# Weight sums of two pairs in single slots, sums of x begun earlier, key tiles copied by one engine

## The chip, the cores and the metric

The program runs on one NeuronCore of a Trainium2 chip, with float32 inputs and outputs. Five engines run side by side: TensorE (PE in the views; PEld is its weight load), VectorE (DVE), ScalarE (ACT), GpSimd (POOL) and SyncE (SP, which here only issues transfers). The metric is the device time of one execution in microseconds; a kernel is told by the median of its runs.

## What is computed

Two layers of one mixer, on x of 512 rows by 1024. `jnp.split(z, ...)` cuts one wide projection into three token mixers, three gate paths and the merge logits.

```python
for l in range(DEPTH):                                   # 2
    z = jnp.einsum('bsd,de->bse', x, w_in[l])
    (q_lat, kv_lat, k_pe, g_mla, lru_u, g_lru,
     r_q, r_k, r_v, g_ret, merge_logits) = jnp.split(z, IN_SPLITS, axis=-1)
    y_mla = _mla(...) * jax.nn.silu(g_mla)               # attention, 8 heads, keys from a latent
    y_lru = _rglru(...) * jax.nn.silu(g_lru)
    y_ret = _retention(r_q, r_k, r_v, ...) * jax.nn.silu(g_ret)
    gates = jax.nn.sigmoid(merge_logits + b_merge[l]).reshape(B, S, N_BRANCHES, D_MODEL)
    mixed = (gates[:, :, 0] * jnp.einsum('bse,ed->bsd', y_mla, w_branch[l, 0])
             + gates[:, :, 1] * jnp.einsum('bse,ed->bsd', y_lru, w_branch[l, 1])
             + gates[:, :, 2] * jnp.einsum('bse,ed->bsd', y_ret, w_branch[l, 2]))
    out = jnp.einsum('bsd,de->bse', mixed, w_out[l])
    x = _layer_norm(DEEPNORM_ALPHA * x + out, ln_g[l], ln_b[l])
```

## The kernel before

**Products.** A float32 product is made of three matmuls of a shorter float type (`mm3`, L138 to L140): each operand is split into a high part, a cast by ScalarE (L113), and the rest, a subtraction by VectorE (L114). Weights arrive in raw tiles (`wr`, `ws`) and leave as `wh` and `wl`.

**Stages of a layer.** Latent projections, the recurrence, the attention (query tiles, then four key tiles `psk`, L641 to L645, whose two heads each are copied to `kt` by VectorE, L644, and by ScalarE, L645), the retention, and then 14 pairs of tiles for the merge gates and one gate path, each gate pair with its branch projection `psb`, and the output projection.

**The retention** is the loop of six passes at L791. Pass q makes tile q of keys and queries (`ret_in`: two projections into `psmm`, each turned by `rope`, four VectorE operations whose temporaries `rsw` and `rt` are slots), then for tile q-1 the transposes, scores `sd` and states (`ret_keys`, `ret_states`), then for tile q-2 the output (`ret_out`, into `por`, copied to `yr` by ScalarE at L789). The values `vr` lie in a wide tile and are read by the last `por`. In passes 4 and 5 the loop also makes the sums of x, two steps each.

**The pairs.** `in_pair` (L445) makes two tiles of 512 columns as seven block products in place of eight, in the way of Strassen and Winograd: into `psx`, `psy1` and `psz`, from blocks of x and of the weights and from sums of such blocks. The sums of x are common to all pairs: `x_sums` (L329) builds them in a scratch tile `sx` by VectorE additions (L341, L344; four chunks of 256 columns at once) and splits them into `tx` and, the last, into a free part of `xth`, `xtl`. The first gate pair needs them one after another. Between products ScalarE or VectorE fetches `psx`; the copy L468 is one such fetch, and the next product into `psx` waits for it.

**The sums of weights** are made per pair by `Blocks` (L370). `load` issues on SyncE the two raw halves `ws` (L395, L396), then on GpSimd an accumulating transfer that adds a third block to them (L398 for both halves at once, 512 KB; L401 one half each, 256 KB), and on SyncE the raw tiles `wr` (L405, L409 for the branch weights `wbr`, L412). `make` splits one block after another in the order a11, a12, s1, s2, b1, s3, b0, a22, s4; the cast of s1 is the first to read the accumulated `ws`. Casts run up to six blocks (`AHEAD`) in front of the products. Pair 0 has its raw sums in two slots. Pairs 1, 2, 3, ... share one wide tile, `self.two`, half of it each.

**What sets the order.** Tiles come from pools: 13 slots of 128 x 512, five wide tiles (four slots each), four half ones, three `wr`, four pairs `wh`/`wl`, three PSUM buffers for `psmm`, `por`, `psx` and the like. A tile waits until the last reader of its buffer's former content is done. The order on each engine is the order of the program with priorities: weight loads and their splits are pulled forward (L840 for the first pair). Every engine works strictly in its order, so an instruction that waits holds up all behind it.

Of the kernel before, what the change touches and what calls it, by code (L numbers as in the profile page):

```python
# [12 lines left out]
F32R = mybir.dt.float32r  # L13
# [10 lines left out]
KD = D // P  # L24
# [43 lines left out]
HS = S // 2  # L68
# [5 lines left out]
def trunk(ctx, tc, x_in, xt_in, pos, vecs, wg, wt, wrv, wuq, wuk, wuv, wlru, wbr, wout, lng, lnb, dec, rett, out):  # L74
    nc = tc.nc
# [18 lines left out]
    def slot(name, dt=F32):  # L94
        return tmp.tile([P, S], dt, tag="slot", name=name, bufs=NSLOT)

    def wide(name, dt=F32):
        return tmp.tile([P, NST, S], dt, tag="wide", name=name, bufs=NWIDE)

    def half(name, dt=F32):  # L100
        return tmp.tile([P, 4, S], dt, tag="half", name=name, bufs=4)

    def PS(n):
        if n in SS:
            return ps_s.tile([P, S], F32, tag="s", name=n)
        return ps_mm.tile([P, S], F32, tag="mm", name=n)

    def raw(t):
        return t.bitcast(F32)


    def split(hi, lo, src):
        nc.scalar.copy(hi, src)  # L113
        nc.vector.tensor_tensor(out=lo, in0=src, in1=raw(hi), op=ALU.subtract)  # L114
# [51 lines left out]
    def v(l, col, n=1):  # L166
        return vec[:, l * NV + col:l * NV + col + n]
# [139 lines left out]
    def layer(l):  # L307
# [13 lines left out]
        tx = [None] * 4  # L321
# [4 lines left out]
        def sums(i):  # L326
            return [(tx[i][0][:, j, :], tx[i][1][:, j, :]) for j in range(HK)]

        def x_sums(t1, t2, t3, scratch):  # L329


            tx[:3] = [(t[:, :, :HS], t[:, :, HS:]) for t in (t1, t2, t3)]
            tx[3] = (xth[:, :HK, HS:], xtl[:, :HK, HS:])
            r1, r2 = scratch[:, :, :HS], scratch[:, :, HS:]

            def b(k, t):
                o = (slice(None), slice(HK * k, HK * k + HK), slice(HS * t, HS * t + HS))
                return raw(xth[o]), raw(xtl[o])

            def sub(out, a, c, op=ALU.subtract):  # L340
                nc.vector.tensor_tensor(out=out, in0=a, in1=c, op=op)  # L341

            def neg_less(out, a, c):
                nc.vector.scalar_tensor_tensor(out=out, in0=a, scalar=-1.0, in1=c[0], op0=ALU.mult, op1=ALU.subtract)  # L344
                sub(out, out, c[1])

            def less(out, a, c):
                sub(out, a[0], c[0])
                sub(out, out, a[1], ALU.add)
                sub(out, out, c[1])  # L350

            def one():
                less(r1, b(0, 0), b(0, 1))
                split(tx[0][0], tx[0][1], r1)

            def two():
                neg_less(r2, r1, b(1, 1))
                split(tx[1][0], tx[1][1], r2)

            def three():  # L360
                less(r1, b(1, 1), b(0, 1))
                split(tx[2][0], tx[2][1], r1)

            def four():
                neg_less(r2, r2, b(1, 0))
                split(tx[3][0], tx[3][1], r2)

            return [one, two, three, four]

        class Blocks:  # L370
# [10 lines left out]
            def load(self):  # L381
                n = self.loaded
                if n == len(self.pairs):
                    return
                self.loaded += 1
                t, wb = self.pairs[n]
                d = {}
                if n == 0:
                    s0, s1 = slot("ws0"), slot("ws0")
                elif n == 1:  # L390
                    self.two = wide("ws")
                if n:
                    s = self.two[:, n % 2 * 2:n % 2 * 2 + 2, :]
                    s0, s1 = s[:, 0, :], s[:, 1, :]
                nc.sync.dma_start(out=s0, in_=wt[l, t + 1][:, 512:])  # L395
                nc.sync.dma_start(out=s1, in_=wt[l, t][:, :512])  # L396
                if n:
                    nc.gpsimd.dma_start(out=s, in_=wt[l, t + 1][:, :512].unsqueeze(1).to_broadcast([P, 2, 512]), accum_op=ALU.add)  # L398
                else:
                    for sn in (s0, s1):  # L400
                        nc.gpsimd.dma_start(out=sn, in_=wt[l, t + 1][:, :512], accum_op=ALU.add)  # L401
                d["s1"] = d["s2"] = d["s4"] = s0
                d["s3"] = s1
                r = wraw.tile([P, 1024], F32, tag="wr", name="wr")
                nc.sync.dma_start(out=r, in_=wt[l, t])  # L405
                d["a11"], d["a12"] = r[:, :512], r[:, 512:]
                if wb is not None:
                    r = wraw.tile([P, 1024], F32, tag="wr", name="wr")
                    nc.sync.dma_start(out=r, in_=wb)  # L409
                    d["b0"], d["b1"] = r[:, :512], r[:, 512:]  # L410
                d["a22"] = slot("wr2")
                nc.sync.dma_start(out=d["a22"], in_=wt[l, t + 1][:, 512:])  # L412
                self.raws.append(d)
# [110 lines left out]
        for g in range(2 if l else 0):  # L524
            chunks = lat_weights(l, g)
            if g == 0:
                for st in range(NST):
                    ps = PS("psg0")
# [25 lines left out]
        for c in range(4):  # L554
            ps = in_tile(T_U + c)
            cw = V_CW + 4 * c
            nc.vector.tensor_scalar(out=xc[:, c, :], in0=ps, scalar1=v(l, cw + 3), scalar2=v(l, V_CB + c), op0=ALU.mult, op1=ALU.add)
            for j in range(3):
                d = 3 - j
# [3 lines left out]
        for b in range(5):  # L563
            ps = ps_t.tile([P, S], F32, tag="t", name="psl")
# [11 lines left out]
        ps = ps_t.tile([P, S], F32, tag="t", name="pskp")  # L576
# [5 lines left out]
        for b in range(8):  # L582
            c = b // 2
            q, o = (slice(0, 64), slice(64, 128)) if b % 2 == 0 else (slice(64, 128), slice(0, 64))
# [3 lines left out]
            ps = PS("psr")  # L588
# [29 lines left out]
        kt = [kth[h // 4][:, h % 4, :] for h in range(H)]  # L618
# [3 lines left out]
        for c in range(3):  # L622
            hi, lo = load_w(wuq[l, c], 768)
            for j in range(2):
                t = 2 * c + j
                ps = PS("psq2" if t % 2 else "psq")
# [12 lines left out]
        for t in range(4):  # L639
            ps = PS("psk")  # L640
            for k in range(2):  # L641
                w = slice((t * 2 + k) * P, (t * 2 + k + 1) * P)
                mm3(ps, (hi[:, w], lo[:, w]), kvlat[k], k == 0, k == 1)
            nc.vector.tensor_copy(kt[2 * t][0:64, :], ps[0:64])  # L644
            nc.scalar.copy(kt[2 * t + 1][0:64, :], ps[64:128])  # L645
        hi, lo = load_w(wuv[l], 1024)
        for st in range(NST):
            sl = slice(st * P, (st + 1) * P)
            ps = PS("psvm")
# [71 lines left out]
        steps = [(h, i) for h in range(H) for i in range(NST)]  # L721
# [22 lines left out]
        def ret_in(t):  # L744
            rts[t] = half("rt")
            rope(rts[t][:, 1, :], in_tile(T_RK + t), cos_r, sin_r)
            rope(rts[t][:, 0, :], in_tile(T_RQ + t), cos_r, sin_r)
# [43 lines left out]
        for q in range(6):  # L791
            if q < 4:
                ret_in(q)
            if 0 <= q - 1 < 4:
                ret_keys(q - 1)
                ret_states(q - 1)
            if 0 <= q - 2 < 4:
                ret_out(q - 2)
            if q >= 4:
                if q == 4:  # L800
                    steps = x_sums(wide("tx", F32R), wide("tx", F32R), half("tx", F32R), half("sx"))
                steps[2 * q - 8]()
                steps[2 * q - 7]()


        mixed = [slot("mixed") for _ in range(KD)]
        mixhl = {}

        def branch_mm(w, j, ys):
# [34 lines left out]
        def gate_pair(b, d2, ys, mh=None):  # L844
            gts = [slot("gt") for _ in range(2)]
            bias = [v(l, V_BM + b * KD + 2 * d2 + j) for j in range(2)]
            psb = {}

            def gate(i, part, src):
                if i == 0:  # L850
                    nc.scalar.activation(gts[0], gts[0], AF.Sigmoid, bias=bias[0])
                    return
                nc.scalar.activation(gts[1][:, part], src, AF.Sigmoid, bias=bias[1], scale=-1.0)
                nc.scalar.activation(gts[1][:, HS:], gts[1][:, HS:], AF.Sigmoid, bias=bias[1], scale=-1.0)

            def branch(j):
                psb[j] = branch_mm(bs.take(), 0, ys)

            in_pair(bs, gts, gate, branch)
            for j in (1, 0):  # L860
                d, gt = 2 * d2 + j, gts[j]
                if b == 1:
                    nc.vector.tensor_tensor(out=mixed[d], in0=psb[j], in1=gt, op=ALU.mult)
                    continue
                nc.vector.tensor_tensor(out=gt, in0=psb[j], in1=gt, op=ALU.mult)
                nc.vector.tensor_tensor(out=mixed[d], in0=mixed[d], in1=gt, op=ALU.add)
                if b == 2:
                    ml = slot("ml", F32R)
                    split(mh[:, d % 4, :], ml, mixed[d])
                    mixhl[d] = (mh[:, d % 4, :], ml)  # L870
# [41 lines left out]
        for d2 in range(4):  # L912
            if d2 % 2 == 0:
                mh = half("mh", F32R)
            if d2 in (1, 2):
                t = tmp.tile([P, 2, 1024], F32, tag="wide", name="wor", bufs=NWIDE)
# [8 lines left out]
        for n, c in enumerate(WO):  # L925
            if c in WO_W:
                dst = None
            elif c in WO_X:
                t = tmp.tile([P, 2, 1024], F32R, tag="wide", name="wow", bufs=NWIDE)
# [18 lines left out]
        for st in range(NST):  # L948
# [11 lines left out]
            for g, (c0, c1) in enumerate(cuts):  # L960
                n = c1 - c0
                if pss:
                    ps = pss[g]
                    out_mm(ps, sl, c0, n, (KD - 1, KD - 2), (False, True))
                else:
                    ps = ps_mm.tile([P, S], F32, tag="mm", name="pso")[:, :n]
# [18 lines left out]
    for l in range(DEPTH):  # L985
        layer(l)
# [85 lines left out]
```

## Time and profile before

| | |
|---|---|
| median of 3 runs | 1059.83 us (1059.24 to 1062.46) |
| the profiled execution | 1059.59 us |
| its span, first to last instruction | 1057.8 us |
| busy: PE, PEld, DVE, ACT, POOL | 97%, 86%, 78%, 51%, 10% |
| chain that ended last: PE, DVE, ACT, issue, DMA | 76%, 10%, 8%, 3%, 3% |
| mean granted TensorE clock | 0.993 |

Busy time is an average over stages that differ. A stage is read from its waits: a wait of PE names the engine and the line that ended it, the timeline gives its place, and the chain of waits tells what that one waited for in turn. The granted clock is 1.00 at 2.4 GHz and 0.50 at 1.2 GHz; a window's value is the mean.

### The profile page before, as it was taken

To read this page: it belongs to the slowest core of one execution; us is meant where nothing else is said; L and a number is where in the kernel's file an instruction comes from. 1 tells how busy PE (TensorE), PEld (TensorE's weight loads), DVE (VectorE), ACT (ScalarE), POOL (GpSimd) and SP (SyncE) were. 2 spreads that over 40 slices of the span, in tenths; PEclk is the share of its full clock that TensorE was granted. 3 is DMA by queue.
4 is the path that set the end of the run, shared out by engine and by line. 5 is a ranking of instruction groups with operands and counts; after the bars stand their busy time and mean duration, and the time that the engine had idled before them with its cause. 6 is when DMAs were issued, how large, how long until landed. Compare 5 with 4: busy or idle time off the path is not lost.

```text
span 1057.8 us, 16761 instructions
## 1 busy us (share of the span) xinstructions
PE 1029.3 (97%) x6279; PEld 907.2 (86%) x6279; DVE 821.3 (78%) x1608; ACT 539.5 (51%) x1025; POOL 109.0 (10%) x161
## 2 busy tenths in 40 slices
PE   9999999999699999999999999999998999999997
PEld 8878788889599999998898787888887999999986
DVE  6988988667796787787646888985688877877765
ACT  4659577621555465463124695775225555555610
POOL 1200012100002200100002000121000022001000
PEclk9999999999899999999999999999999999999999
DMA  8612523552476556545136225136516754666311
GB/s 256 170 70 85 160 81 81 123 118 59 120 210 169 150 159 189 144 136 172 63 131 158 80 81 168 56 81 149 117 34 166 207 149 141 165 210 170 125 64 60
DMA packets 52081, 138.26 MB, mean 131 GB/s; under 512 B 5664, under 2 KB 8608, under 8 KB 52000
## 3 DMA queue, kind: packets, MB, share of 16 engines
q1 hardware_dynamic: 39744, 106.44, 30.3%
q0 software_dynamic: 11968, 30.41, 16.4%
q8 instruction: 49, 0.80, 0.3%
q10 hardware_dynamic: 288, 0.34, 0.2%
q14 instruction: 32, 0.26, 0.1%
HBM read 130.88 MB, written 4.19 MB: 128 GB/s over the span
## 4 chain that ended last, share of the span: by engine, by line
PE 76%; DVE 10%; ACT 8%; issue 3%; DMA 3%; SPq 0%; DVEq 0%; ACTq 0%; POOLq 0%
PE psx L138 5%; PE psx L139 5%; PE psx L140 5%; PE psmm L138 5%; PE psmm L140 5%; PE psmm L139 5%; PE psb L138 4%; PE psb L139 4%; PE psb L140 4%; PE pso L139 3%; PE pso L140 3%; PE pso L138 3%; PE psz L138 3%; PE psz L140 2%; PE psz L139 2%
## 5 line engine op out<-in xcount | busy, mean ns | idle before, releaser
L113 ACT CAST wh<-wr 128x512 fp32r<-128x512 f32 (+5 forms) x188 | 133.5, 723 | 124.4 <-PE psmm L139 42.2
L114 DVE TENSOR_TENSOR wl<-wr,wh 128x512 fp32r<-128x512 f32 (+5 forms) x188 | 151.8, 818 | 30.3 <-ACT wh L113 29.6
L138 PE MATMUL psmm<-xth,wh 128*128 128x512 f32 x320 | 125.9, 393 | 0.0
L139 PE MATMUL psmm<-xtl,wh 128*128 128x512 f32 x320 | 125.1, 391 | 0.0
L140 PE MATMUL psmm<-xth,wl 128*128 128x512 f32 x320 | 124.7, 390 | 0.0
L113 ACT CAST wh<-ws 128x512 fp32r<-128x512 f32 x112 | 69.4, 620 | 89.6 <-PE psx L139 38.5
L114 DVE TENSOR_TENSOR wl<-ws,wh 128x512 fp32r<-128x512 f32 x112 | 77.1, 689 | 43.9 <-ACT wh L113 43.0
L138 PE MATMUL psx<-xth,wh 128*128 128x256 f32 x224 | 65.3, 292 | 10.2 <-ACT gt L468 10.1
L140 PEld LDWEIGHTS psmm<-xth,wl 128*128 128x128 f32 x320 | 60.1, 188 | 12.5
L138 PEld LDWEIGHTS psmm<-xth,wh 128*128 128x128 f32 x320 | 60.1, 188 | 12.2
L139 PEld LDWEIGHTS psmm<-xtl,wh 128*128 128x128 f32 x320 | 60.1, 188 | 11.8
L138 PE MATMUL psx<-tx,wh 128*128 128x256 f32 x224 | 64.2, 286 | 2.5 <-ACT tx L113 2.3
L139 PE MATMUL psx<-xtl,wh 128*128 128x256 f32 x224 | 64.6, 288 | 0.0
L140 PE MATMUL psx<-xth,wl 128*128 128x256 f32 x224 | 63.9, 287 | 0.0
L140 PE MATMUL psx<-tx,wl 128*128 128x256 f32 x224 | 63.4, 283 | 0.0
L139 PE MATMUL psx<-tx,wh 128*128 128x256 f32 x224 | 63.3, 283 | 0.0
L398 POOL DMA_DIRECT2D ws<-in_wt x26 | 31.2, 1200 | 305.9 <-DMA ws<-in_wt 233.5
L138 PEld LDWEIGHTS psx<-xth,wh 128*128 128x128 f32 x224 | 43.7, 195 | 12.9 <-ACT gt L468 11.1
L138 PEld LDWEIGHTS psx<-tx,wh 128*128 128x128 f32 x224 | 42.8, 191 | 6.1 <-ACT tx L113 3.2
L139 PEld LDWEIGHTS psx<-xtl,wh 128*128 128x128 f32 x224 | 44.1, 197 | 1.0
L139 PEld LDWEIGHTS psx<-tx,wh 128*128 128x128 f32 x224 | 42.8, 191 | 1.3
L140 PEld LDWEIGHTS psx<-xth,wl 128*128 128x128 f32 x224 | 43.6, 195 | 0.2
(310 smaller groups left out, 3079.3 us busy)
## 6 DMA issues: line engine op xcount, KB each, us to landing
wr<-in_wt SPq DMA_DIRECT2D x68, 512.0 KB, 3.7
ws<-in_wt SPq DMA_DIRECT2D x56, 256.0 KB, 3.0
ws<-in_wt POOLq DMA_DIRECT2D x26, 512.0 KB, 6.7
wr<-in_wbr SPq DMA_DIRECT2D x24, 512.0 KB, 4.6
wl<-in_wt POOLq DMA_DIRECT2D x22, 512.0 KB, 6.3
wr<-in_wt SPq DMA_DIRECT2D x28, 256.0 KB, 3.6
wr<-in_wrv SPq DMA_DIRECT2D x8, 512.0 KB, 3.3
wor<-in_wout SPq DMA_DIRECT2D x8, 512.0 KB, 5.8
```

The costliest lines, as they stand in the source:

```text
L113: nc.scalar.copy(hi, src)
L114: nc.vector.tensor_tensor(out=lo, in0=src, in1=raw(hi), op=ALU.subtract)
L138: nc.tensor.matmul(ps, lh, rh, start=start, stop=False, skip_group_check=more)
L139: nc.tensor.matmul(ps, lh, rl, start=False, stop=False, skip_group_check=more)
L140: nc.tensor.matmul(ps, ll, rh, start=False, stop=stop, skip_group_check=more)
L398: nc.gpsimd.dma_start(out=s, in_=wt[l, t + 1][:, :512].unsqueeze(1).to_broadcast([P, 2, 512]), accum_op=ALU.add)
```

## The change

Three things. The raw weight sums of pair 1, like those of pair 0, are put in two slots with an accumulating transfer each; the wide tile begins with pair 2. `x_sums` takes its tiles one after another where they are first written and is spread over passes 2 to 5 of the retention, one step each, with the steps cut a little differently. The VectorE copy of the key tiles becomes a ScalarE copy. Also, the slots of `mixed` are taken when they are written.

```diff
-        def x_sums(t1, t2, t3, scratch):
-            tx[:3] = [(t[:, :, :HS], t[:, :, HS:]) for t in (t1, t2, t3)]
+        def x_sums(scratch):
             tx[3] = (xth[:, :HK, HS:], xtl[:, :HK, HS:])
...
+            def parts(i, t, r):
+                tx[i] = (t[:, :, :HS], t[:, :, HS:])
+                split(tx[i][0], tx[i][1], r)
             def one():
                 less(r1, b(0, 0), b(0, 1))
-                split(tx[0][0], tx[0][1], r1)
+                parts(0, wide("tx", F32R), r1)
+                neg_less(r2, r1, b(1, 1))
             def two():
-                neg_less(r2, r1, b(1, 1))
-                split(tx[1][0], tx[1][1], r2)
+                less(r1, b(1, 1), b(0, 1))
             def three():
-                less(r1, b(1, 1), b(0, 1))
-                split(tx[2][0], tx[2][1], r1)
+                parts(2, half("tx", F32R), r1)
+                parts(1, wide("tx", F32R), r2)
...
-                if n == 0:
+                if n < 2:
                     s0, s1 = slot("ws0"), slot("ws0")
-                elif n == 1:
+                elif n == 2:
                     self.two = wide("ws")
-                if n:
+                if n >= 2:
                     s = self.two[:, n % 2 * 2:n % 2 * 2 + 2, :]
...
-                if n:
+                if n >= 2:
                     nc.gpsimd.dma_start(out=s, in_=wt[l, t + 1][:, :512].unsqueeze(1).to_broadcast([P, 2, 512]), accum_op=ALU.add)
                 else:
                     for sn in (s0, s1):
...
-            nc.vector.tensor_copy(kt[2 * t][0:64, :], ps[0:64])
+            nc.scalar.copy(kt[2 * t][0:64, :], ps[0:64])
             nc.scalar.copy(kt[2 * t + 1][0:64, :], ps[64:128])
...
-            if q >= 4:
-                if q == 4:
-                    steps = x_sums(wide("tx", F32R), wide("tx", F32R), half("tx", F32R), half("sx"))
-                steps[2 * q - 8]()
-                steps[2 * q - 7]()
-        mixed = [slot("mixed") for _ in range(KD)]
+            if q == 2:
+                steps = x_sums(half("sx"))
+            if q >= 2:
+                steps[q - 2]()
+        mixed = {}
...
                 if b == 1:
+                    mixed[d] = slot("mixed")
                     nc.vector.tensor_tensor(out=mixed[d], in0=psb[j], in1=gt, op=ALU.mult)
```

The changed kernel's lines stand some three to five lower from there on (L398 and L399 load `ws`, L404 accumulates one half, L471 is the copy that was L468).

SyncE's queue in the last passes of layer 1's retention, before (`ws_2808` and `ws_2809` are pair 0's slots, `ws` the wide tile; `wr_2818` and `wr_2903` are the second raw tiles of pairs 0 and 1):

```order
L395 DMA ws_2808<-in_wt 128x512
L396 DMA ws_2809<-in_wt 128x512
L412 DMA wr_2818<-in_wt 128x512
L412 DMA wr_2903<-in_wt 128x512
L395 DMA ws<-in_wt 128x512
L396 DMA ws<-in_wt 128x512
L395 DMA ws<-in_wt 128x512
L396 DMA ws<-in_wt 128x512
L409 DMA wr<-in_wbr 128x1024
```

and now (`ws_2800`, `ws_2801` for pair 0, `ws_2887`, `ws_2888` for pair 1):

```order
L398 DMA ws_2800<-in_wt 128x512
L399 DMA ws_2801<-in_wt 128x512
L415 DMA wr_2810<-in_wt 128x512
L398 DMA ws_2887<-in_wt 128x512
L399 DMA ws_2888<-in_wt 128x512
L415 DMA wr_2897<-in_wt 128x512
L398 DMA ws<-in_wt 128x512
L399 DMA ws<-in_wt 128x512
L398 DMA ws<-in_wt 128x512
L399 DMA ws<-in_wt 128x512
L412 DMA wr<-in_wbr 128x1024
```

Pair 1's two loads stand ahead of the wide tile's, which are now those of pairs 2 and 3; the loads into `ws_2887` and `ws_2888` wait for reads of rope temporaries on VectorE. Pair 1's branch weights stay behind all of them.

VectorE in the retention, from the scores `sd` of one tile to the next rope, before (`state_120`: that tile's states):

```order
L764 TENSOR_TENSOR sd<-psrs,tabs 128x512 x2
L775 COPY state_120<-pskv 64x64
L755 TENSOR_TENSOR rt<-rt,tabs 128x384
L777 SCALAR_TENSOR_TENSOR state_120<-state_120,retd,pskv 64x64 x2
L775 COPY state_120<-pskv 64x64
L777 SCALAR_TENSOR_TENSOR state_120<-state_120,retd,pskv 64x64 x2
L234 STREAM_SHUFFLE rsw<-psmm 128x512
```

and now, from the same `sd` to the same rope:

```order
L767 TENSOR_TENSOR sd<-psrs,tabs 128x512 x2
L778 COPY state_120<-pskv 64x64
L340 TENSOR_TENSOR sx<-sx,xtl 128x4x256
L780 SCALAR_TENSOR_TENSOR state_120<-state_120,retd,pskv 64x64
L343 SCALAR_TENSOR_TENSOR sx<-sx,xth 128x4x256
L780 SCALAR_TENSOR_TENSOR state_120<-state_120,retd,pskv 64x64
L778 COPY state_120<-pskv 64x64
L114 TENSOR_TENSOR tx<-sx,tx 128x4x256
L780 SCALAR_TENSOR_TENSOR state_120<-state_120,retd,pskv 64x64
L340 TENSOR_TENSOR sx<-sx,xtl 128x4x256
L780 SCALAR_TENSOR_TENSOR state_120<-state_120,retd,pskv 64x64
L234 STREAM_SHUFFLE rsw<-psmm 128x512
```

Three sums and a split have come in between the states of one tile and the rope of the next (the rope that starts at 244.51 us in the trace of before).

ScalarE around the copy L468 (now L471) of pair 0, before:

```order
L113 CAST wh<-ws 128x512
L113 CAST xth<-sx 128x4x256
L468 COPY gt<-psx 128x256
L113 CAST wh<-wr 128x512
L853 ACT_TABLE_LOAD
```

and now:

```order
L113 CAST xth<-sx 128x4x256
L113 CAST wh<-wr 128x512
L113 CAST wh<-ws_2800 128x512
L113 CAST wh<-wr_2810 128x512
L113 CAST wh<-wr 128x512
L113 CAST wh<-ws_2800 128x512
L467 COPY gt<-psx 128x256
L113 CAST wh<-wr 128x512
L113 CAST wh<-ws_2887 128x512
L471 COPY gt<-psx 128x256
L113 CAST wh<-wr 128x512
```

The cast of the last sum of x (`xth<-sx`) has moved ahead of most of pair 0's casts; the cast of pair 1's s1 still stands in front of the copy, and reads a slot now.

## Rows read from the trace of the kernel before

**Rows 1.** The page's first part: busy us, share of the span, instructions.

```profile
PE 1029.3 (97%) x6279; PEld 907.2 (86%) x6279; DVE 821.3 (78%) x1608; ACT 539.5 (51%) x1025; POOL 109.0 (10%) x161
```

**Rows 2.** Waits of PE: waiter, what ended the wait, us in total, times, longest.

```profile
PE psx L138 <- ACT gt L468: 10.1, 2, 6.4
PE psx L138 <- ACT tx L113: 2.3, 2, 1.2
PE psb L140 <- DVE wl L114: 2.1, 2, 1.0
PE psk L138 <- ACT kt L645: 1.4, 2, 0.7
```

**Rows 3.** Timeline of PE: start, us, what, [idle before it and its releaser].

```profile
277.64 0.40 PE L138 MATMUL psb<-yl,wh 128*128 128x512 f32 x1
277.88 0.39 PE L139 MATMUL psb<-yl,wh 128*128 128x512 f32 x1
...
285.02 0.58 PE L138 MATMUL psx<-xth,wh 128*128 128x256 f32 x1 [6.40 <-ACT gt L468]
...
808.00 0.58 PE L138 MATMUL psx<-xth,wh 128*128 128x256 f32 x1 [3.67 <-ACT gt L468]
```

**Rows 4.** The chain that ended last, 250 to 300 us: start, us, what.

```profile
269.47 4.61 DMA ws<-in_wt
...
274.61 8.50 DMA ws<-in_wt
...
283.65 1.04 ACT xth L113
```

**Rows 5.** Timeline of ScalarE, 283 to 301 us.

```profile
283.13 0.62 ACT L113 CAST wh<-ws 128x512 fp32r<-128x512 f32 x1 [6.61 <-DMA ws<-in_wt]
...
284.60 0.36 ACT L468 COPY gt<-psx 128x256 f32<-128x256 f32 x1
...
299.74 0.38 ACT L468 COPY gt<-psx 128x256 f32<-128x256 f32 x1 [1.05 <-PE psx L140]
```

**Rows 6.** Windows: us, busy us per engine (instructions), granted clock, DMA share, GB/s.

```profile
250.00:255.00 5.00, 5.00 (x48) 4.72 (x46) 5.00 (x10) 1.04 (x1) 0.00 (x0) 1.00 0.01 3
...
285.00:290.00 5.00, 4.98 (x25) 4.77 (x26) 4.89 (x8) 2.75 (x5) 0.00 (x0) 0.63 0.01 1
805.00:810.00 5.00, 2.00 (x7) 1.78 (x8) 2.29 (x3) 3.64 (x5) 0.00 (x0) 0.75 0.85 193
810.00:815.00 5.00, 5.00 (x40) 5.00 (x40) 4.40 (x9) 2.88 (x6) 0.00 (x0) 0.91 0.00 0
```

**Rows 7.** Timeline of VectorE in the retention and the first gate pair.

```profile
233.73 0.01 DVE L234 LOAD_MASK_SELECT rsw<-psmm  x1 [1.47 <-PE psmm L140]
...
244.51 0.01 DVE L234 LOAD_MASK_SELECT rsw<-psmm  x1 [4.64 <-PE psmm L140]
...
248.49 2.48 DVE L341 TENSOR_TENSOR sx<-sx,xtl 128x1024 f32<-128x1024 f32 x2
...
267.75 0.29 DVE L777 SCALAR_TENSOR_TENSOR state<-state,retd,pskv 64x64 f32<-64x64 f32 x1
...
274.47 1.23 DVE L114 TENSOR_TENSOR tx<-sx,tx 128x1024 fp32r<-128x1024 f32 x1
```

**Rows 8.** Waits of SyncE's queue, 200 to 300 us, columns as in rows 2.

```profile
SPq L395 <- PE por L788: 21.4, 1, 21.4
```

**Rows 9.** Timeline of GpSimd, 225 to 300 us.

```profile
274.61 1.21 POOL L398 DMA_DIRECT2D ws<-in_wt  x1 [31.99 <-DMA ws<-in_wt]
```

**Rows 10.** Transfers by issue, 225 to 300 us: count, KB each, median us to landing.

```profile
ws<-in_wt POOLq DMA_DIRECT2D x2, 256.0 KB, 5.0
```

**Rows 11.** Timeline of PE at the keys; instructions on `kt`: ns lowest/median/highest.

```profile
128.54 0.50 PE L138 MATMUL psk<-lh,wh 128*128 128x512 f32 x1 [0.72 <-ACT kt L645]
...
L644 DVE COPY kt<-psk x8: 671/682/685, 127.2 to 656.0; 64x512 f32<-64x512 f32 x8
L645 ACT COPY kt<-psk x8: 575/582/583, 127.9 to 657.2; 64x512 f32<-64x512 f32 x8
```

## Prediction

> **What bounds the kernel now.** I read the page's busy line first: PE is busy 1029.3 of 1057.8 us [rows 1], so the kernel can gain where TensorE stands still or runs at its lower clock, and hardly anywhere else. Next come the waits of PE, grouped by what ended them [rows 2]. Four groups are worth more than 1.3 us, each has two members (one per layer), and together they hold 10.1 + 2.3 + 2.1 + 1.4 = 15.9 us. Three of them stand in the first two gate pairs after the retention, the fourth in the key projection of the attention. The reader should then find the largest in the timeline: a 6.40 us hole before 285.02 in layer 1 and a 3.67 us hole before 808.00 in layer 2 [rows 3]. The matmul behind each hole takes 0.58 us, and the windows say why: the granted clock is 0.63 as a mean over 285 to 290 us, and 0.75 and 0.91 over 805 to 815 [rows 6], where the stretches ahead have 1.00. So a hole costs its length and some time at the lower level (1.2 GHz) behind it.
>
> What fills the hole is in the chain [rows 4]: SyncE's load of the raw halves of pair 1 starts only at 269.47 and takes 4.61 us, GpSimd's accumulating transfer starts at 274.61 and takes 8.50 us. ScalarE's cast of that sum starts at 283.13 after 6.61 us of nothing, and behind it on the same engine stand the cast of the last sum of x (1.04 us) and the copy L468 that TensorE needs [rows 4, 5]. Why the issue is so late is in SyncE's waits: 21.4 us for the last `por` of the retention [rows 8], since the wide tile takes over the buffer of `vr`, which is read until then.
>
> **1. Pair 1 in slots.** It removes one 512 KB accumulating transfer per layer and adds two of 256 KB; SyncE's two loads stay. The loads no longer wait for `vr`: a slot comes free when a rope temporary has been read. By the order of the changed kernel these are two ropes of the last passes: before, the first ends at 247.3 us (one 1.22 us sum ahead of the two from 248.49, [rows 7]), the second, one rope on, at 253.4. Chain: 253.4 + 4.61 + 0.5 (the gap between landing and issue in [rows 4]) + 5.0 [rows 10] = 263.5 us, with 8.5 [rows 4] in place of 5.0 at worst 267. The cast stands just ahead of the copy (before: L468, 284.6), and TensorE is ready for what follows at 278.6, so the sum is wanted by about 276. Cover: 9 to 12 us. The holes go: 6.40 + 3.67 = **10.1 us**.
>
> The lower clock goes with them. In 285 to 290 PE worked 4.98 us at 0.63: 0.37 x 4.98 = 1.8 us. In layer 2 the 2.00 us busy before 810 ran at half speed (0.58 us matmuls, [rows 3]), 1.0 us, and 0.09 x 5 = 0.45 up to 815: together 1.5. **3.3 us** [rows 6].
>
> A rule that speaks against this part: the Trainium skill (DMA: Bandwidth & Descriptors, SWDGE vs HWDGE vs iDMA) says that GpSimd writes the descriptor rings into SBUF, and GPSIMD Engine Reference (the table of its specifications) says that it shares its SBUF interface with VectorE and contends with VectorE's instructions of two SBUF inputs. Pair 1's issues move from 274.6 to about 251 and 258, where such instructions fill VectorE. The row: VectorE is busy 5.00 of 5 us in 250 to 255 [rows 6], but the issue at 274.61 took 1.21 us while such an instruction ran beside it, from 274.47 for 1.23 us [rows 7, 9]. By the rule the issue could end only behind a run of these, some 5 us later, and the cover still holds; by the row it is free. The sum is the same, the chance of rival A is not.
>
> **2. Sums of x, one step per pass from the third.** Nothing is removed: twelve VectorE operations of 1.22 us per layer and four splits move. What they stand in for: VectorE waits 4.64 us before 244.51 and 1.47 us before 233.73 for `psmm` [rows 7]. The new order puts two sums (2.4 us) before the second of these ropes and three sums and a split (3 x 1.22 + 1.23 = 4.9 us) into the first-named gap, so the rope at 244.51 comes (2.4 - 1.5) + (4.9 - 4.6) = 1.2 us late, and catches up behind it, where three sums (3.7 us) stood and two stand now. Three `mm` buffers lie between rope and TensorE; whether 1.2 us gets through I can't read, so I bound it by 0 and 1.2 per layer.
>
> At the other end, before the last state, the old order has two tx-sized operations, the sums and four operations of pair 0's weights; it ends the state at 268.0 (267.75 + 0.29, [rows 7]). Adding up the new rows from 255.0 by the same durations I get 265, so `por`, and with it the buffer of `vr`, comes about 3 us sooner. The last two products of pair 0 then find their operands made: the wait on the cast of tx (2.3 us, both layers) and that on `wl` of pair 0 (2.1 us), which was queued behind the sums on VectorE, go: **4.4 us** [rows 2]. New short waits at `por` and `psz`, where a sum now stands between states: I bound them by 0 and two sums per layer (2.4 us) and take 0.45, near the lower end, since TensorE had no wait at all on these states before [rows 2].
>
> **3. Keys by ScalarE alone.** VectorE loses four copies of 0.68 us per layer, ScalarE gains four of 0.58 [rows 11]. A tile of keys is two copies, 1.16 us in a row, against the 6 matmuls of TensorE; matmuls of this size start 0.24 us apart (277.64 and 277.88, [rows 3]), so a tile takes 1.4 us. Before, ScalarE's copies waited for VectorE's, busy with a weight split and a rope, and TensorE waited 0.72 us for a buffer [rows 11]. Now the copy starts when the matmuls end, but the last weight cast (1.04 us at that size, [rows 4]) stands among them. Bounds: a gain of 1.4 (all of it) and a loss of 1.0 per layer (that cast). I take a gain of **1.2**, since only one cast comes in eight copies.
>
> **4. The `mixed` slots** taken one by one cost no instruction; they leave slots free in pair 0 and so let the loads of later pairs go sooner, behind nothing that TensorE waits for.
>
> **What is late next.** Pairs 2 and 3 keep the wide tile and the wait for the last `por`. From 265.5: 0.4 + 4.61 + 0.5 + 8.50 = 279.5 us. ScalarE's cast of it now stands ahead of pair 1's copy L468, which ran at 299.74 [rows 5] and would run at 289 after a gain of 10.4: cover 9 us.
>
> **Sum.** 10.1 + 3.3 + 4.4 + 1.2 - 0.9 (new waits, two layers) = 18.1 us against the profiled run, 1059.59, which is 0.24 from the median: **1041.5 us**, 1.7% faster.
>
> A second look at the price of the accumulating transfer: the Trainium skill (DMA: Bandwidth & Descriptors, Anatomy of one DMA) gives a fit of 2.0 us plus bytes by 436 GB/s, an estimate of 3.2 us for 512 KB and 2.6 us for 256 KB. The rows have 8.50 and 5.0 [rows 4, 10]; by the fit pair 1 would be there 2.4 us sooner, pair 2 some 5 us sooner, and the sum would not move.
>
> **Rivals.**
> A. *A new hole takes part of it back.* Pair 1's branch weights (`wbr`) still stand behind the four wide loads in SyncE's queue, and pair 2's sum still behind `por`; with the wide transfers at once, a landing could be late by more than its cover, with ScalarE's copies queued behind the cast. A hole of 2 to 4 us per layer and half as much at the lower clock (the 3.67 us hole brought 1.5): 2 x 3 + 2 = 8 us back: 1049. For: the head-of-line place is the same. Against: 9 us of cover. 0.12.
> B. *The hole only moves to pair 2.* That takes pair 2's sum landing 6.4 us after it is wanted, at 295, 16 us behind my sum; then only the small waits and the keys are gained, 4.4 + 1.2: about 1054. For: SyncE's 21.4 us wait for `por` stays. Against: pair 2 is wanted one pair, 14 us, later. 0.04.
> C. *Slower: VectorE becomes the bound of the retention.* If the sums between ropes and states are paid in full by TensorE (seven of the twelve operations stand before or among them: 7 x 1.22 + 1.23 = 9.8 us per layer) and the key casts lose 1.0 each, 2 x 10.8 = 21.6 is lost and 18.1 + 0.9 - 1.2 = 17.8 gained: about 1063. It decides once VectorE's gaps before the ropes (1.5 + 4.6 us, [rows 7]) don't take the sums; 6.1 us of gaps meet 7.3 us of work there, the 1.2 us of part 2. 0.02.
> D. *It doesn't do what it says*: the slots come as late as `vr` did, since 13 slots must hold two more tiles. Then the hole stays and the time is 1059.6 - 5 = 1054 with the parts 2 and 3, or 1059 without. The order names ropes as releasers, so 0.02.
>
> **How the numbers follow.** Forecast 0.80, around 1041.5: all gains without any new wait (18.1 + 0.9 + 0.2) give 1040.4, and an earlier `psx` (by the 3 us at which the states end) could give 1 to 3 more: 1038. With the upper bounds of the new waits (2 x 3.6 in place of 0.9) and the keys at -2.0, 1051; half-way there, 1046. The range 1037.5 to 1048.5 holds the forecast and the better half of A, some 0.83. A measurement tells about 0.3% (3.2 us) from no change. Faster: forecast, A and B and most of D, 0.95; same 0.03; slower 0.02.
>
> **What would show it.** Right: no PE wait on L468's successor above 1 us; clock 1.00 in all windows of the first gate pairs; pair 1's four transfers landed before 268 us; no `psb` or `tx` wait; SyncE's wait for `por` now with pairs 2 and 3 alone. Wrong: a wait of ScalarE's cast on `DMA ws` ahead of a copy of psx (A, B); waits of PE on `state`, `sd` or `rt` between 228 and 268 (C); a key wait above 0.7 us per layer (part 3).

## The result and the profile after

The changed kernel takes 1042.0 us as a median of four runs (1040.3 to 1042.68); the kernel before, on the same chip, 1060.28 (four runs). The ratio is 0.982, with a 95% interval of 0.980 to 0.984. The forecast was 1041.5 us in a range of 1037.5 to 1048.5. A second comparison on another chip, with nine runs of the kernel before (median 1062.27), gave 1041.49 us and 0.981 (0.979 to 0.982): 20.8 us less by the medians, where the forecast had 18.1.

The first parts of the page of the changed kernel answer to [rows 1]: the span fell by 19.3 us, TensorE's share rose from 97% to 99%.

```profile
span 1038.5 us, 16757 instructions
...
PE 1024.3 (99%) x6279; PEld 904.5 (87%) x6279; DVE 817.4 (79%) x1600; ACT 544.6 (52%) x1033; POOL 109.8 (11%) x163
...
PE 90%; ACT 4%; DVE 4%; issue 1%; DMA 1%; SPq 0%; DVEq 0%; ACTq 0%
```

The last line is the chain that ended last: PE 90%, where it had 76%, and DMA 1% where it had 3%. The waits of PE (waiter, what ended the wait, us in total, times, longest) answer to [rows 2]:

```profile
PE warm L147 <- DVE idle L144: 1.5, 1, 1.5
PE por L788 <- DVE state L780: 1.4, 2, 0.7
PE po L715 <- ACT pth L113: 1.0, 3, 0.4
...
PE psz L138 <- ACT yr L792: 0.2, 1, 0.2
```

All four groups of [rows 2] are gone. In their place there is one new group of more than a few tenths, the outputs `por` of the retention that wait for a state, 0.7 us per layer. The windows, us, busy us of PE, PEld, DVE, ACT and POOL (instructions), granted clock, DMA share, GB/s, answer to [rows 6]:

```profile
245.00:250.00 5.00, 5.00 (x32) 4.16 (x32) 4.97 (x8) 0.00 (x0) 0.00 (x0) 1.00 0.20 61
250.00:255.00 5.00, 5.00 (x47) 4.71 (x46) 4.64 (x10) 0.70 (x2) 0.86 (x1) 1.00 0.54 123
255.00:260.00 5.00, 5.00 (x48) 4.88 (x45) 4.83 (x12) 1.73 (x3) 0.86 (x1) 1.00 0.44 87
260.00:265.00 5.00, 4.31 (x38) 4.17 (x36) 4.15 (x8) 4.64 (x9) 0.00 (x0) 1.00 0.00 0
...
275.00:280.00 5.00, 5.00 (x41) 4.88 (x40) 5.00 (x11) 3.73 (x6) 0.00 (x0) 1.00 1.09 190
280.00:285.00 5.00, 5.00 (x41) 4.87 (x40) 4.87 (x10) 3.54 (x7) 0.00 (x0) 1.00 0.87 261
285.00:290.00 5.00, 5.00 (x29) 4.37 (x28) 5.00 (x11) 1.22 (x3) 0.00 (x0) 1.00 0.47 139
```

Where the old trace had the hole and the clock at 0.63, TensorE is busy 5.00 of 5 us at 1.00. The issues of SyncE and then of GpSimd (start, us, what) show why:

```profile
246.69 0.33 SPq L398 DMA_DIRECT2D ws<-in_wt  x1
252.02 0.33 SPq L399 DMA_DIRECT2D ws<-in_wt  x1
...
265.38 0.33 SPq L398 DMA_DIRECT2D ws<-in_wt  x1
...
250.02 0.86 POOL L404 DMA_DIRECT2D ws<-in_wt  x1 [8.10 <-DVE rsw L234]
256.25 0.86 POOL L404 DMA_DIRECT2D ws<-in_wt  x1 [5.36 <-DVE state L778]
270.26 1.21 POOL L401 DMA_DIRECT2D ws<-in_wt  x1 [13.15 <-DMA ws<-in_wt]
```

Pair 1's accumulating transfers are issued at 250 and 256 us, where its only one was issued at 274.61 before [rows 9]. The one at 270.26 is now pair 2's. ScalarE's timeline about the copy that was L468 [rows 5]:

```profile
272.36 0.62 ACT L113 CAST wh<-ws 128x512 fp32r<-128x512 f32 x1
273.73 0.37 ACT L471 COPY gt<-psx 128x256 f32<-128x256 f32 x1 [0.75 <-PE psx L140]
...
287.00 0.62 ACT L113 CAST wh<-ws 128x512 fp32r<-128x512 f32 x1 [2.19 <-PE psb L139]
288.61 0.37 ACT L471 COPY gt<-psx 128x256 f32<-128x256 f32 x1 [0.99 <-PE psx L140]
```

The copies wait for TensorE, no longer TensorE for them. The cast at 287.00, pair 2's, waited for TensorE too and not for its transfer.

### The profile page after: what moved, and what is told of

Read it like the earlier page. It is cut to its first block, busy times and chain, and to the rows that moved or that the text cites. A ratio compares the mean times of both kernels' runs of the same rounds, so it can differ in the third digit from the quotient of the medians.

```text
span 1038.5 us, 16757 instructions
## 1 busy us (share of the span) xinstructions
PE 1024.3 (99%) x6279; PEld 904.5 (87%) x6279; DVE 817.4 (79%) x1600; ACT 544.6 (52%) x1033; POOL 109.8 (11%) x163
## 4 chain that ended last, share of the span: by engine, by line
PE 90%; ACT 4%; DVE 4%; issue 1%; DMA 1%; SPq 0%; DVEq 0%; ACTq 0%
PE psmm L140 7%; PE psmm L139 7%; PE psmm L138 7%; PE psx L138 5%; PE psx L139 5%; PE psx L140 5%; PE psb L138 4%; PE psb L139 4%; PE psb L140 4%; PE pso L138 3%; PE pso L139 3%; PE pso L140 3%; PE psz L138 3%; PE psz L140 3%; PE psz L139 3%; PE psg L139 2%
## 5 line engine op out<-in xcount | busy, mean ns | idle before, releaser
L401 POOL DMA_DIRECT2D ws<-in_wt x24 | 28.8, 1201 | 258.0 <-DMA ws<-in_wt 197.7
L684 ACT ACTIVATE pr<-pss,nm 128x128 f32<-128x128 f32 (+1 forms) x64 | 34.0, 533 | 17.7 <-DVE nm L679 14.6
```

The lines of the kernel that those rows point to most:

```text
L684: nc.scalar.activation(pr[:, :n], ps[:, :n], AF.Exp, bias=nm, scale=-1.0, accum_out=rs)
```

## The experiments

Ratios are against the kernel before, run on the same chip beside each; one thousandth is 1.06 us. In the three sets its median was 1062.66, 1062.22 and, for the last two runs, 1062.27 us. A difference in us is worked out from the ratio.

### Each part alone

**Slots alone.** The kernel before, with:

```diff
-                if n == 0:
+                if n < 2:
                     s0, s1 = slot("ws0"), slot("ws0")
-                elif n == 1:
+                elif n == 2:
                     self.two = wide("ws")
-                if n:
+                if n >= 2:
...
-                if n:
+                if n >= 2:
```

and with the slots of `mixed` taken one by one.

> The kernel before with pair 1's raw sums in slots (and the slots of mixed taken one by one); sums of x and keys as before. Theory (the hole is the late issue alone): the 6.4 and 3.7 us holes and the 3.3 us at the lower clock go, the waits on tx (2.3), on wl (2.1) and at the keys (1.4) stay: 13.4 us faster, about 1046.5. Rival (the hole has a second filling: the last sum of x, cast in front of the same copy L468, ends on VectorE at 276.8): a hole of 1 to 3 us per layer stays, with its stretch at the lower clock, and the gain is 7 to 11 us.

Measured: 1046.83 us, ratio 0.985 (0.984 to 0.986), 16 us faster. The waits of PE on the copy are gone and those on tx (2.3), wl (2.0) and the keys (1.5) stay, as the theory had it. The rival filling was there and came just in time:

```profile
276.46 1.05 ACT L113 CAST xth<-sx 128x1024 fp32r<-128x1024 f32 x1
277.40 0.37 ACT L468 COPY gt<-psx 128x256 f32<-128x256 f32 x1
```

This is ScalarE's timeline of this kernel: the last sum of x is cast, and the copy stands right behind it. TensorE had no wait on it.

**Sums alone.** The kernel before, with the new `x_sums` and

```diff
-            if q >= 4:
-                if q == 4:
-                    steps = x_sums(wide("tx", F32R), wide("tx", F32R), half("tx", F32R), half("sx"))
-                steps[2 * q - 8]()
-                steps[2 * q - 7]()
+            if q == 2:
+                steps = x_sums(half("sx"))
+            if q >= 2:
+                steps[q - 2]()
```

> The kernel before with the sums of x begun in the third pass; pair 1 in the wide tile and the keys as before. Theory: the waits on tx and wl go (4.4 us), waits of 0.7 us per layer on the last states come (as in the changed kernel), the hole keeps its length within 1 us, since the last por and TensorE's need move forward alike: 3 us faster, 1 to 5. Rival (the early end of the retention itself shortens the hole, since it frees vr's buffer 3 to 4 us sooner): the holes shrink by 2 to 3 us each and the gain is 7 to 10 us.

Measured: 1053.24 us, ratio 0.991 (0.988 to 0.993), 10 us faster: the rival's figure. The hole is there still. The profiled execution, 1056.72 us, was the slowest of the six (1048.62 the fastest), and shows it at 4.12 us in layer 1, where it was 6.40, and at 4.41 in layer 2, where the trace of before had 3.67. From the waits of PE of this kernel:

```profile
PE psx L138 <- ACT gt L471: 8.5, 2, 4.4
...
PE por L788 <- DVE state L780: 1.4, 2, 0.7
```

and from its chain that ended last, through the hole in layer 1 (start, us, what):

```profile
266.89 3.37 DMA ws<-in_wt
...
270.80 9.26 DMA ws<-in_wt
...
280.61 0.37 ACT gt L471
```

The chain has lost the cast of the last sum of x, 1.04 us, which stood between the cast of ws and the copy before [rows 4, 5] and is now made long ahead. And the retention ends sooner (SyncE's load starts at 266.89, not 269.47).

**Keys alone.** The kernel before, with

```diff
-            nc.vector.tensor_copy(kt[2 * t][0:64, :], ps[0:64])
+            nc.scalar.copy(kt[2 * t][0:64, :], ps[0:64])
```

> The kernel before with the VectorE copies of the key tiles on ScalarE. Theory: TensorE's 0.72 us wait per layer goes and nothing follows it: 1.4 us faster, and the trace has no wait of PE on kt. Rival: what is gained there is waited for in the attention or at the hole, and the time is the same within 0.5 us.

Measured: 1061.21 us, ratio 0.998 (0.997 to 0.999), 2.3 us faster. The interval, 1 to 4 us, holds the 1.4 us of the waits of PE too; what tells the two apart is in the traces. From the first key matmul to the start of the rope that stood at 228.36 us, this kernel takes 1.04 us less than the kernel before, and 1.26 us less at the same place in layer 2: 2.3 us together. The timelines of PE over the keys, first of the kernel before, show two interruptions:

```profile
127.43 0.39 PE L139 MATMUL psvm<-wl,lh 128*128 128x512 f32 x1
...
133.00 0.38 PE L674 MATMUL pss<-kt,qt 96*128 96x128 f32 x2
133.45 0.50 PE L138 MATMUL psvm<-wh,lh 128*128 128x512 f32 x1
```

then of this kernel:

```profile
132.04 0.39 PE L138 MATMUL psvm<-wh,lh 128*128 128x512 f32 x1
132.27 0.39 PE L139 MATMUL psvm<-wl,lh 128*128 128x512 f32 x1
132.50 0.39 PE L140 MATMUL psvm<-wh,ll 128*128 128x512 f32 x1
132.72 1.46 PE L674 MATMUL pss<-kt,qt 96*128 96x128 f32 x6
```

Before, 127.43 is followed by the matmul at 128.54 [rows 11]. That is 1.11 us between starts that are else 0.23 apart: 0.88 lost where the wait shows 0.72. A second stumble follows at 133.00, where the scores start before the values are complete. With ScalarE's copies the key and value matmuls run at 0.23 us without a break.

### Each part undone

The changed kernel with one of the three edits taken back; with the slots, `mixed` is taken at once again too.

> The changed kernel with pair 1's raw sums back in the wide tile (and mixed taken at once). If the three parts add up, this costs the 13.4 us of the two holes and their lower clock: about 1055.5, 4.8 us under the kernel before. If the earlier end of the retention shortens the hole by itself: 7 to 10 us under the kernel before.

Measured: 1050.18 us, ratio 0.990 (0.988 to 0.991): 11 us under the kernel before, where adding up had 4.8. From the waits of PE:

```profile
PE psx L138 <- ACT gt L471: 5.1, 2, 3.1
```

and the matmul behind the hole of layer 1 in the timeline of PE:

```profile
279.00 0.38 PE L138 MATMUL psx<-xth,wh 128*128 128x256 f32 x1 [3.15 <-ACT gt L471]
```

The hole is 3.15 us where it was 6.40 [rows 3], and 1.93 in layer 2, where it was 3.67. So the parts overlap: the earlier sums shorten the hole that the slots remove.

> The changed kernel with the sums of x back in passes 4 and 5, two steps each. If the parts add up: waits on tx and wl come back (4.4 us), the 1.4 us at por go: 3 us slower than the changed kernel, about 1045. If the sums of x are a second filling of the hole (the last one ends at 276.8 and is cast in front of the copy that TensorE needs): 5 to 9 us slower than the changed kernel.

Measured: 1044.52 us, ratio 0.983 (0.982 to 0.985). Against the changed kernel's 0.981 to 0.982 that is 1 to 3 us slower, the first expectation. Its waits are tx 2.3 and wl 2.1, and none on the copy: once the slots are there, the sums of x don't fill the hole again.

> The changed kernel with the key copies shared by VectorE and ScalarE as before. Theory: 1.4 us slower than the changed kernel (0.72 per layer, a wait of PE on kt). Rival: the same within 0.5 us.

Measured: 1043.93 us, ratio 0.984 (0.982 to 0.986), 1.5 and 3.4 us slower than the changed kernel by its two ratios; the waits of PE have psk at 1.4 again.

The remaining edit, the slots of `mixed` taken one by one, comes with the slots of pair 1 in every run. It was not run alone. In the changed kernel it moves nothing in the program: with all eight taken at once the instructions of every engine stand in the same order and wait for the same ones.

### Is pair 2 covered?

The changed kernel with pair 2 in slots as well (the two conditions that follow, `n >= 2`, become `n >= 3`, and the wide tile's halves are counted from pair 3):

```diff
-                if n < 2:
+                if n < 3:
                     s0, s1 = slot("ws0"), slot("ws0")
-                elif n == 2:
+                elif n == 3:
                     self.two = wide("ws")
...
```

> The changed kernel with pair 2's raw sums in slots as well; the wide tile begins with pair 3. Theory (pair 2 has about 8 us of cover, so its wait for the last por costs nothing): the same within 1 us. Rival 1 (the hole has moved to pair 2 in a small way): 1 to 3 us faster. Rival 2 (13 slots are too few for two more raw sums): 1 to 6 us slower, with waits of VectorE or ScalarE for a slot.

Measured: 1057.26 us, ratio 0.996 (0.994 to 0.997): 15 us slower than the changed kernel, far beyond the 1 to 6 us of the second rival. The hole is back, at pair 2. From the timelines of SyncE, GpSimd, ScalarE and PE:

```profile
279.89 0.33 SPq L412 DMA_DIRECT2D wr<-in_wbr  x1
281.38 0.33 SPq L408 DMA_DIRECT2D wr<-in_wt  x1
281.80 0.38 SPq L398 DMA_DIRECT2D ws<-in_wt  x1
...
289.79 1.75 POOL L404 DMA_DIRECT2D ws<-in_wt  x2 [15.93 <-DVE mu L823]
...
294.26 0.62 ACT L113 CAST wh<-ws 128x512 fp32r<-128x512 f32 x1 [9.31 <-DMA ws<-in_wt]
294.78 0.37 ACT L471 COPY gt<-psx 128x256 f32<-128x256 f32 x1
...
295.20 0.58 PE L138 MATMUL psx<-xth,wh 128*128 128x256 f32 x1 [3.74 <-ACT gt L471]
...
817.95 0.58 PE L138 MATMUL psx<-xth,wh 128*128 128x256 f32 x1 [4.93 <-ACT gt L471]
```

In the changed kernel pair 2's loads are issued at 265.38, ahead of pair 1's branch weights. Here they stand in SyncE's queue behind the branch weights of pairs 1 and 2 and the raw tiles of 2 and 3, and go at 281.80. They land late too, among five other transfers (DMA by issue, 278 to 296 us: count, KB each, median us to landing):

```profile
ws<-in_wt SPq DMA_DIRECT2D x2, 256.0 KB, 7.5
ws<-in_wt POOLq DMA_DIRECT2D x2, 256.0 KB, 4.9
```

The cast then has 9.31 us of waiting in front of the same copy. The profile puts the end of GpSimd's wait to VectorE (`mu`), but the first load lands at about the same time (281.80 + 7.5 = 289.3). The wide tile, not the slot, was the early place for pair 2. Why the order puts the slot loads so late isn't settled, and "13 slots are too few" was only argued: no run has more.

### The wait that is left

The changed kernel with the sums one pass earlier still:

```diff
-            if q == 2:
+            if q == 1:
                 steps = x_sums(half("sx"))
-            if q >= 2:
-                steps[q - 2]()
+            if 1 <= q <= 4:
+                steps[q - 1]()
```

> The changed kernel with the sums of x one pass earlier still, in passes 1 to 4. Theory: the 0.7 us wait per layer of the last por on the states goes, since no sum stands between these states: up to 1.4 us faster than the changed kernel. Rival (the sums now stand in front of ropes and states of the early passes, where VectorE has 2 us gaps at most, or take a half tile that the ropes' results need): new waits of PE on rt or on a buffer of 1 to 5 us per layer, and slower than the changed kernel by 1 to 8 us.

Measured: 1043.03 us, ratio 0.982 (0.980 to 0.983), the same as the changed kernel. Neither expectation names the outcome. The waits of PE:

```profile
PE psy L138 <- ACT gt L855: 1.1, 2, 0.8
...
PE psz L138 <- DVE gt L478: 1.0, 2, 0.5
...
PE psz L138 <- ACT wh L113: 0.9, 2, 0.4
```

The wait on the states is gone, and there are 3.0 us of others in the first gate pairs that the first trace of the changed kernel doesn't have. Then the same edit more gently, two steps in pass 2 and one each in passes 3 and 4, beside the changed kernel on one chip:

```diff
-            if q >= 2:
-                steps[q - 2]()
+            for i in {2: (0, 1), 3: (2,), 4: (3,)}.get(q, ()):
+                steps[i]()
```

> The changed kernel once more, beside the next one and on the same chip. With the holes gone its time should hardly vary: within 0.3% of 1042.0, spread under 3 us, where the kernels with a hole have spread by 5 to 8.

> The changed kernel with the steps of the sums of x in passes 2 (two steps), 3 and 4. Theory: the wait of the last por on the states (0.7 us per layer) comes from the split of tx that stands between two states and waits for its cast; here the last states stand together but for one split, so that wait goes and the time falls by up to 1.4 us. Rival: two sums now stand between the parts of a rope in pass 3, the ropes come 2 to 3 us late, and TensorE waits for a psmm buffer or for rt: 1 to 4 us slower than the changed kernel.

Measured: the changed kernel 1041.49 us (1040.39 to 1042.84), ratio 0.981 (0.979 to 0.982); this one 1042.05 us (1041.4 to 1042.38), 0.981 (0.980 to 0.982). The changed kernel's spread is 2.5 us, under the 3 expected. Between the two kernels there is no difference. `por` waits for no state in the gentler kernel, and TensorE has other waits. But not all of these are new. The second trace of the changed kernel (1042.58 us; the first was its fastest, 1040.3) has, beside the 1.4 us at `por`, two of the three that the trace of the earlier sums has:

```profile
PE psz L138 <- DVE gt L478: 0.9, 2, 0.5
...
PE psy L138 <- ACT gt L855: 0.6, 1, 0.6
```

Only the wait of psz on wh, 0.9 us in both kernels with earlier sums, is in neither trace of the changed kernel. From the first trace's timelines of VectorE and PE, and then from PE's of the gentler kernel:

```profile
261.29 1.23 DVE L114 TENSOR_TENSOR tx<-sx,tx 128x1024 fp32r<-128x1024 f32 x1 [0.67 <-ACT tx L113]
...
264.47 0.49 PE L788 MATMUL por<-state,rt 128*128 128x128 f32 x2 [0.69 <-DVE state L780]
```

```profile
265.06 0.39 PE L138 MATMUL psz<-tx,wh 128*128 128x256 f32 x1 [0.43 <-ACT wh L113]
280.36 0.38 PE L138 MATMUL psy<-xth,wh 128*128 128x256 f32 x1 [0.49 <-ACT gt L855]
282.53 0.39 PE L138 MATMUL psz<-tx,wh 128*128 128x256 f32 x1 [0.48 <-DVE gt L478]
```

VectorE's split of tx waits 0.67 us for its cast on ScalarE and holds up the states behind it, the last of which also has a sum in front of it (262.87 us, 1.23 us); TensorE waits 0.69. Without that, TensorE comes to psz, psy and psz before ScalarE and VectorE are ready, to the last two of these as in the second trace of the changed kernel. In the changed kernel TensorE is busy 59.2 us and VectorE 57.1 of the 60 from 240 to 300 us, so there is little left to shift between them, and no version here beats it.

## Why the prediction was right

The time came out 0.5 us beside the forecast. That it is so near is in part luck: the slots, as the first of the edits, and the keys were each worth one to three us more than priced, and the kernel before ran at 1060.28 us there and at 1062.2 to 1062.7 in the sets of the experiments. The mechanism of the main step held. By its steps:

- **The hole and the lower clock, 13.4 us.** Right in mechanism: both holes and the low windows are gone, the slots alone remove the holes and undoing the slots brings them back. The chain was forecast to end at 263.5. The second accumulating issue came at 256.25, and transfers of its kind and size took a median of 4.2 us, so it landed by about 261. As the first of the edits the slots brought 16 us, not 13.4. The 6.40 + 3.67 us came from one execution, which lay at the lower end of that kernel's runs: its 3.67 us hole in layer 2 was 6.37 in the trace of the kernel with only the keys changed. The accumulating transfer in front of it took 7.37 us in the one and 10.02 in the other: the hole grew by 2.70 us, the transfer by 2.65.
- **The waits on tx and wl, 4.4 us, less 0.9 for new ones.** Right with the slots there (1 to 3 us measured, 4.4 us of waits gone for 1.4 of new ones). What the step didn't say is that the same edit also shortens the hole, so that alone it brings 10 us. In a sum over waits each wait has one owner, and here the hole had two: the late transfer, and the cast of the last sum behind it. The order of the changed kernel showed the second (xth ahead of the casts), and I didn't price it. It did no harm, because the slots removed the hole whole.
- **The keys, 1.2 us.** Undersized, as far as the traces show. The runs gave 2.3 us alone and 1.5 to 3.4 us by undoing, with intervals that hold 1.4 too. In the traces the stretch from the first key matmul to the rope shrinks by 2.3 us in two layers, and by 2.6 between the kernel with the keys undone and the changed one. What failed is the bound of 1.4 us taken from the wait rows; the spacing of the starts shows 0.88 us per layer at that wait and a second interruption behind it.
- **New waits.** 0.7 us per layer at `por`, forecast as 0.45, and in the second trace of the changed kernel 1.5 us more at `psz` and `psy`. A sum does stand between the last two states, as I had it; what I hadn't is the split of tx in front of them waiting 0.67 us for its cast, about as long as TensorE's 0.69. The rope that was to come 1.2 us late started at 243.43, with everything 1.28 us earlier (the rope of 228.36 in the old trace started at 227.08; 1.04 of that come from the keys, the rest lies ahead of them), so 0.2 us late, and TensorE noticed nothing.
- **What is late next.** SyncE's issue behind the last `por` at 265.38 (forecast 265.5), pair 2's sum at 270.26 + 9.0 = 279.3 (279.5), the copy at 288.61 (289). These held because the new order was walked with durations from rows.
- **Rival B** became true in the kernel with three pairs in slots: the hole moved on to pair 2 and the time was 1057, near the 1054 priced for it. It takes pair 2's sum being wanted before it lands, as stated, and an edit one pair further on is enough.
- **The port rule.** The Trainium skill (DMA: Bandwidth & Descriptors, SWDGE vs HWDGE vs iDMA, with GPSIMD Engine Reference, its table of specifications) let one fear that GpSimd's issue is held up by VectorE's two-input instructions. This trace doesn't show it: 0.86 us at 250.02 and at 256.25 beside a VectorE busy 4.64 and 4.83 of 5 us (at 250.20 with `rsw<-rsw,sinr`, two SBUF tiles, for 0.68 us), and 0.87 at 240.06 in the old trace, where VectorE was idle.
- **The fit for the transfers.** The Trainium skill (DMA: Bandwidth & Descriptors, Anatomy of one DMA) gives 2.0 us plus bytes by 436 GB/s, an estimate of 3.2 us for 512 KB and 2.6 for 256 KB. The accumulating transfers of these runs took 8.1 to 9.4 and 4.1 to 5.0 us, as medians of a run, in the retention of layer 1 and the first gate pair, beside other traffic. The measurement decides.

## What to carry to other kernels

A hole in TensorE's timeline is priced by its length, by the time at the lower clock behind it, and by everything that stands in the queue between the late transfer and the copy that TensorE needs; undo the parts singly before giving each a share, since two edits can shorten the same hole. A loaded buffer that is shared with a long-lived tile is late by that tile's last reader: look for a buffer that comes free sooner, but look in the new order where the load then stands in its queue, because one pair further the same edit cost 15 us. Where the waits are short, take what an interruption costs from the spacing of the starts and not from the wait row alone.

## What the runs showed of the hardware

- The spread of a kernel's runs came with the hole. The kernels that have it ran from 1059.21 to 1064.93 us (the kernel before, 17 runs), 1048.62 to 1056.72 (sums alone), 1054.51 to 1059.46 (three pairs in slots); those without it from 1046.57 to 1047.59 (slots alone) and 1044.17 to 1044.8 (sums undone). Two kernels without a hole had one run each some 2 to 3 us above the rest.
- The granted clock was 1.00 through waits of 0.7 us, and through those of 1.0 and 1.2 us in the kernel with the slots alone. Behind the holes of 3.67 us and longer the first matmul took 0.58 us. Behind the one of 3.15 us it took 0.38, and the slower spacing (0.21 us) began about 1 us later. Even the hole of 1.93 us in layer 2 of the kernel with the slots undone had it behind it: the first matmul at 797.33 took 0.39 us, and from 799 to 802 us the granted clock was 0.50, the lower level.
